# Output projection of a two-layer GLA/MLA trunk: seven products of halves per 1024 tokens in place of eight

## The chip, the cores and the metric

One core of one Trainium2 chip runs the whole program. The metric is the device time of one execution in microseconds (us), taken as the median of several runs.

## The reference

Two layers; the change touches only the last line of each:

```python
for l in range(DEPTH):                       # DEPTH = 2
    h = rmsnorm(x, norm_g[l])
    z = h @ w_in[l]                          # split into the parts of two head groups
    ...
    o_gla = gla_mix(...) * silu(g_gate)      # (1, 2048, 512)
    o_mla = block_causal_attention(q, k, v) * silu(m_gate)   # (1, 2048, 512)
    x = x + jnp.concatenate([o_gla, o_mla], axis=-1) @ w_out[l]   # w_out[l]: 1024 x 1024
```

All arrays are float32; x has 2048 tokens of 1024 features.

## The kernel before, in words

A layer has four stages: `pass1` (input projections and the gated linear attention), `pass2` (gates, queries, the output of the first head group), `phase_b` (softmax attention of the second group) and `phase_c` (the output projection, L1179 to L1303). Arrays that pass from stage to stage lie in DRAM: `yd[q]` holds the input of the output projection, transposed, for a quarter `q` of 512 tokens, as 8 blocks `k` of 128 features; `xd[q]` holds the residual stream after a layer, `sd[q]` its sums of squares.

Every matrix product is made of three matmuls (`mm3`, L98 to L101): an operand is split into a high part, rounded by ACT (type float32r), and a low part, the rest, by DVE (`V`) or POOL (`G`); the matmuls are high times high, high times low and low times high. A weight block of 128 x 512 thus costs a load, an ACT operation and a DVE or POOL one; a block of `y` likewise (`ysplit`, L1207).

`phase_c` runs over 4 quarters `q` and in each over 8 blocks `m` of 128 output features. `part` (L1220) makes one block: 8 blocks `k` of input features, three matmuls each, into one of four PSUM banks (`co`). `done` (L1229) evicts it: DVE adds the residual block `xc`, which was loaded from DRAM by `xload`, and stores the sum to `xd` (layer 0) or to the output (layer 1). In layer 0 it also squares the sum on ACT and adds it to `ac` on POOL (L1242). In the first quarter three banks are begun with `k` 0 to 3, whose `y` was split in `phase_b` (`ypre`, L1162).

All of `w_out` is split ahead of the stage, near the end of `phase_b` (`load_wo`, L1121 and L1158 to L1160), into units of 128 x 4 x 512 from a pool of 12 (`unit`, L91). In layer 0 `phase_c` also loads and splits the next layer's weights `mi` and `qk` (`wpieces`, L236, through `wi_pieces`), normalises the first quarter (`norm0`) and makes the first two hidden tiles (`prep_x`, `prep_h`).

The order of TensorE's instructions in `phase_c` is the order of the program (`manual_schedule`, L1310); on DVE, ACT, POOL and on SP, which issues every DMA (L60), a scheduler orders them ahead of the run, by what is ready and which buffers are free. A pool's tile with a tag and `bufs=n` has n buffers, and an instruction that needs a new one waits for the last use of an old one. Pools `wc` and the PSUM pool exist only in `phase_c`; `hp`, whose two `hT` buffers hold hidden tiles, lasts through the kernel.

## Time and profile before

| | |
|---|---|
| median of 3 runs | 2283.54 us (2283.3 to 2286.54) |
| the profiled execution | 2282.41 us |
| its span, first to last instruction | 2280.6 us |
| around the span | 1.8 us |
| granted TensorE clock | 0.997 of full speed |

The profile is one execution; its sums are held against 2282.41 us. Busy times of an engine are sums of its instructions' durations. PE is TensorE's matmuls, PEld its weight loads, SPq the queue of SP, which issues the DMAs. An instruction's line is that of the helper that emits it: the projection's matmuls stand at L99, L100 and L101 with the tile `co`, its evictions at L1231, the splits of `y` at L1210 and L1211. What follows `<-` in brackets is what an idle engine waited for.

### The profile page before, as it was taken

The numbers are of one execution on the slowest core, as the hardware profiler recorded it, in microseconds if no ns is written. First come the engines' busy times: TensorE is split into PE (matmuls) and PEld (weight loads), VectorE is DVE, ScalarE is ACT, GpSimd is POOL, SyncE is SP. The second block draws the span as 40 slices with busy tenths as digits, with TensorE's granted clock in tenths as the row PEclk, the third lists the DMA queues.
The fourth block names the chain that finished last, engine by engine and source line by source line (L and its number), as shares of the span: only waits on it lengthen the run. The fifth ranks groups of instructions, "written<-read, shape, count | busy, mean of one in ns | idle before, by whom it ended". The sixth has DMA issues, their size and how long they took to land.

```text
span 2280.6 us, 37201 instructions
## 1 busy us (share of the span) xinstructions
PE 2230.0 (98%) x12597; PEld 1927.8 (85%) x12597; DVE 1443.4 (63%) x4421; ACT 1321.4 (58%) x3624; POOL 424.2 (19%) x627
## 2 busy tenths in 40 slices
PE   7999999999999999999999999999999999999999
PEld 5788888888899998888878888888888999988887
DVE  5565557676788888632345555677778888785221
ACT  6655456766777777632244445567777777676100
POOL 0000002334221112232200000044342222123000
PEclk9999999999999999999999999999999999999999
DMA  5410124443311111275421011244432111113542
GB/s 194 142 48 32 43 67 137 127 139 96 107 32 52 36 42 56 65 221 176 139 93 47 29 47 42 71 144 140 124 100 89 37 46 42 36 53 107 178 134 83
DMA packets 168607, 204.78 MB, mean 90 GB/s; under 512 B 12560, under 2 KB 123232, under 8 KB 168416
## 3 DMA queue, kind: packets, MB, share of 16 engines
q1 hardware_dynamic: 168416, 202.40, 28.1%
q8 instruction: 100, 1.64, 0.3%
q14 instruction: 91, 0.75, 0.1%
HBM read 138.39 MB, written 63.96 MB: 89 GB/s over the span
## 4 chain that ended last, share of the span: by engine, by line
PE 86%; ACT 5%; DVE 4%; DMA 3%; issue 1%; POOL 1%; SPq 0%; ACTq 0%; POOLq 0%; DVEq 0%
PE tp L96 8%; PE co L101 5%; PE co L99 5%; PE co L100 5%; PE sp L987 3%; PE sp L990 3%; PE sp L991 3%; PE gt L101 3%; PE gt L100 3%; PE gt L99 3%; PE sp L988 2%; PE o L1062 2%; PE sp L989 2%; PE o L1061 2%; PE mg L101 2%; PE mg L99 2%
## 5 line engine op out<-in xcount | busy, mean ns | idle before, releaser
L100 PE MATMUL co<-y,wo_h 128*128 128x512 f32 x512 | 199.5, 390 | 0.4 <-POOL y L1168 0.4
L99 PE MATMUL co<-y,wo_h 128*128 128x512 f32 x512 | 199.7, 390 | 0.0
L101 PE MATMUL co<-y,wo_l 128*128 128x512 f32 x512 | 199.4, 389 | 0.0
L998 DVE TENSOR_SCALAR_CACHE_REDUCE p<-sp 128x512 f32<-128x512 f32 (+5 forms) x304 | 173.2, 574 | 21.9 <-PE sp L991 18.0
L1005 ACT ACTIVATE p<-p,nm 128x128 f32<-128x128 f32 (+15 forms) x128 | 153.8, 1202 | 36.2 <-DVE nm L1004 31.1
L1040 ACT ACTIVATE ph<-tp 128x512 fp32r<-128x512 f32 x224 | 130.4, 593 | 75.5 <-PE tp L96 67.1
L1041 DVE TENSOR_TENSOR pl<-tp,ph 128x512 fp32r<-128x512 f32 x224 | 151.9, 687 | 33.9 <-ACT ph L1040 32.6
L1060 PE MATMUL o<-ph,v 128*128 128x256 f32 x576 | 168.2, 292 | 4.6 <-ACT ph L1040 3.1
L1062 PE MATMUL o<-pl,v 128*128 128x256 f32 x576 | 170.5, 296 | 2.0 <-DVE pl L1041 1.5
L1231 DVE TENSOR_TENSOR xc<-co,xc 128x512 f32<-128x512 f32 x64 | 44.2, 690 | 202.4 <-PE co L101 201.1
L96 PE MATMUL tp<-cst,p 128*128 128x128 f32 x1088 | 166.2, 275 | 0.5 <-DVE pl L1041 0.2
L1061 PE MATMUL o<-ph,v 128*128 128x256 f32 x576 | 161.4, 280 | 0.0
L186 POOL TENSOR_TENSOR ropeu<-kpe,cos 128x256 f32<-128x256 f32 x8 | 6.8, 846 | 715.0 <-DVE Z L549 714.7
L987 PE MATMUL sp<-kn,q 128*128 128x512 f32 (+3 forms) x320 | 129.6, 405 | 7.1 <-ACT q L922 4.9
L96 PEld LDWEIGHTS tp<-cst,p 128*128 128x128 f32 x1088 | 124.8, 141 | 8.9 <-ACT p L1005 1.3
L1060 PEld LDWEIGHTS o<-ph,v 128*128 128x128 f32 x576 | 109.3, 190 | 12.2 <-ACT ph L1040 5.3
L988 PE MATMUL sp<-kn,q 128*128 128x512 f32 (+3 forms) x320 | 116.5, 364 | 0.0
L989 PE MATMUL sp<-kn,q 128*128 128x512 f32 (+3 forms) x320 | 116.5, 370 | 0.0
L990 PE MATMUL sp<-kr,q 128*128 128x512 f32 (+3 forms) x320 | 115.2, 367 | 0.8 <-ACT q L937 0.4
L1062 PEld LDWEIGHTS o<-pl,v 128*128 128x128 f32 x576 | 109.0, 189 | 7.6 <-DVE pl L1041 3.4
L991 PE MATMUL sp<-kr,q 128*128 128x512 f32 (+3 forms) x320 | 114.2, 367 | 0.0
L100 PEld LDWEIGHTS co<-y,wo_h 128*128 128x128 f32 x512 | 96.2, 188 | 20.8 <-POOL y L1168 0.9
(282 smaller groups left out, 6734.2 us busy)
## 6 DMA issues: line engine op xcount, KB each, us to landing
yst<-yd SPq DMA_DIRECT2D x28, 512.0 KB, 5.0
qd<-qs SPq DMA_DIRECT2D x32, 384.0 KB, 2.9
gst<-qd SPq DMA_DIRECT2D x64, 192.0 KB, 2.5
xn<-in_x SPq DMA_DIRECT2D x16, 512.0 KB, 3.3
od<-osn SPq DMA_DIRECT2D x32, 256.0 KB, 2.1
hf<-in_xt SPq DMA_DIRECT2D x16, 512.0 KB, 3.5
on<-od SPq DMA_DIRECT2D x32, 256.0 KB, 2.7
yd<-yT SPq DMA_DIRECT2D x32, 256.0 KB, 2.8
```

The source lines that it names most:

```text
L96: T.transpose(o, i, ident[:k, :k])
L99: T.matmul(o, lhsT=lh, rhs=rh, start=start, stop=False)
L100: T.matmul(o, lhsT=lh, rhs=rl, start=False, stop=False)
L101: T.matmul(o, lhsT=ll, rhs=rh, start=False, stop=stop)
L987: T.matmul(o, lhsT=qn[:, 0, ts_], rhs=kn[:, 0, k0:k1], start=True, stop=False)
L988: T.matmul(o, lhsT=qn[:, 0, ts_], rhs=kn[:, 1, k0:k1], start=False, stop=False)
L990: T.matmul(o, lhsT=qrr[:, 0, ts_], rhs=kr[:, c0:c1], start=False, stop=False)
L991: T.matmul(o, lhsT=qrr[:, 1, ts_], rhs=kr[:, c0:c1], start=False, stop=True)
L998: V.tensor_scalar(out=pt[:, c0:c0 + w], in0=sp[:, 0:w], scalar1=0.0, scalar2=-3e38, op0=ALU.add, op1=ALU.max, accum_out=mx[:, m:m + 1])
L1060: T.matmul(o[:, s], lhsT=vh, rhs=ph[:, j, s], start=(kb == 0), stop=False)
L1061: T.matmul(o[:, s], lhsT=vl, rhs=ph[:, j, s], start=False, stop=False)
L1062: T.matmul(o[:, s], lhsT=vh, rhs=pl[:, j, s], start=False, stop=(last and j == 1))
```

## The change

The 1024 x 1024 weight is cut into four quarters A11, A12, A21, A22 (input half by row, output half by column; the first input half is scaled by a gain `g`), and the input for 1024 tokens, a pair of quarters q0, q1, into the four halves of 512 features by 512 tokens. Seven products of a weight combination and an input combination take the place of eight: M1 (A11), M5 (S1), M6 (N2), M7 (S3), M3 (S4), M2 (A12), M4 (A22), in this order (`prods`, `left`).

Each product has 4 output blocks `i`, 4 blocks `k` and three matmuls each, `k` outermost (in the very last product `i`). M1, M6, M7 and M4 use the same four banks (`ca`), the first fresh, the others adding to what stands there; M5 and M3 use four others (`cb`), M3 adding; M2 starts those afresh. Every product is evicted by DVE with an added operand: after M1, M5 and M6 a residual block is added and the sum goes to a scratch array `sc` in DRAM; after M7, M3 and M2 the operand is that scratch block, read back, and the sum is final; after M4 the operand is a residual block and the sum final.

Of the weights only A11 and S1 are made in `phase_b`; N2, S3, S4, A12 and A22 are made during the first pair, block by block (`n2`, `s3`, `s4`, `a22`), each from `w_out` loaded anew. The right sides are made and split (`right`, `rput`) one product ahead; the raw halves `ra`, `rb` of `y` are loaded into the two `hT` buffers and are changed in place, other blocks come through `cload`. The next layer's weights are loaded one block at a time, with every second block on POOL alone (the condition in `wpieces`), in the second pair.

The core of the diff, without the removed body of `phase_c`:

```diff
-                    if lo is G and k % 2 == 1:
+                    if lo is G and (k0 + k) % 2 == 1:
...
-            def load_wo(c, half, lo=None):
-                wo[c] = wchunk(lambda hf, k0: bpl.tile([P, 512], F32, tag="stg", name="stg", bufs=NSTG).unsqueeze(1),
-                               1, w_out[l], [(0, c * 512, 512)], 512, f"wo{c}_{l}", ("gla", sm["glag"]), lo,
-                               us=wo.get(c), halves=(half,))
+            def wtile():
+                return bpl.tile([P, 512], F32, tag="stg", name="stg", bufs=NSTG)
+            def load_a11():
+                us = wchunk(lambda hf, k0: wtile().unsqueeze(1), 1, w_out[l], [(0, 0, 512)], 512, f"A11{l}",
+                            ("gla", sm["glag"]), G, halves=(0,))
+                wo["A11"] = us["h", 0], us["l", 0]
+            def load_s1():
+                hi, lo = wo["S1"] = unit([P, 4, 512], F32R, f"S1h{l}"), unit([P, 4, 512], F32R, f"S1l{l}")
+                for k in range(4):
+                    t, u = wtile(), wtile()
+                    dma(t, w_out[l][k * P:(k + 1) * P, 512:1024])
+                    dma(u, w_out[l][512 + k * P:512 + (k + 1) * P, 512:1024])
+                    V.scalar_tensor_tensor(out=u, in0=t, scalar=sm["glag"], in1=u, op0=ALU.mult, op1=ALU.add)
+                    A.activation(out=hi[:, k, :], in_=u, func=AF.Copy)
+                    G.tensor_tensor(out=lo[:, k, :], in0=u, in1=hi[:, k, :].bitcast(F32), op=ALU.subtract)
...
-                    load_wo(0, 0, G)
+                    load_a11()
...
-            load_wo(0, 1, G)
-            load_wo(1, 0)
-            load_wo(1, 1, G)
+            load_s1()
...
     def phase_c(l, wc, pp, yu):
         more = l + 1 < DEPTH
         if more:
             layer_g8(l + 1)
             layer_small(l + 1)
+        g = smalls[l]["glag"]
+        hT01, ac = {}, {}
+        rh, ops, banks = {}, {}, {}
+        prods = ["M1", "M5", "M6", "M7", "M3", "M2", "M4"]
+        left = {"M1": "A11", "M5": "S1", "M6": "N2", "M7": "S3", "M3": "S4", "M2": "A12", "M4": "A22"}
+        W = wo
+        def wtile():
+            return wc.tile([P, 512], F32, tag="ws", name="ws", bufs=6)
+        def wload(c, r):
+            t = wtile()
+            dma(t, w_out[l][r * P:(r + 1) * P, c * 512:(c + 1) * 512])
+            return t
+        def wput(name, k, t, lo, scale=None):
+            hi, ll = W[name][0][:, k, :], W[name][1][:, k, :]
+            if scale is None:
+                A.activation(out=hi, in_=t, func=AF.Copy)
+                lo.tensor_tensor(out=ll, in0=t, in1=hi.bitcast(F32), op=ALU.subtract)
+            else:
+                A.activation(out=hi, in_=t, func=AF.Copy, scale=scale)
+                V.scalar_tensor_tensor(out=ll, in0=t, scalar=scale, in1=hi.bitcast(F32), op0=ALU.mult,
+                                       op1=ALU.subtract)
+        def wmake(name):
+            if name not in W:
+                new = (lambda n: wc.tile([P, 4, 512], F32R, tag="wx", name=n, bufs=2)) if name == "A22" else \
+                    (lambda n: unit([P, 4, 512], F32R, n))
+                W[name] = new(f"{name}h{l}"), new(f"{name}l{l}")
+        def n2(k):
+            wmake("N2")
+            t = wload(0, k)
+            V.scalar_tensor_tensor(out=t, in0=t, scalar=g, in1=W["S1"][0][:, k, :].bitcast(F32), op0=ALU.mult,
+                                   op1=ALU.subtract)
+            V.tensor_tensor(out=t, in0=t, in1=W["S1"][1][:, k, :].bitcast(F32), op=ALU.subtract)
+            wput("N2", k, t, G)
+        def s3(k):
+            wmake("S3")
+            t, u = wload(0, k), wload(1, k)
+            G.tensor_tensor(out=t, in0=t, in1=u, op=ALU.subtract)
+            wput("S3", k, t, None, g)
+        def s4(k):
+            wmake("A12")
+            wmake("S4")
+            t = wload(0, 4 + k)
+            wput("A12", k, t, G)
+            for part in range(2):
+                G.tensor_tensor(out=t, in0=t, in1=W["N2"][part][:, k, :].bitcast(F32), op=ALU.add)
+            wput("S4", k, t, G)
+        def a22(k):
+            wmake("A22")
+            wput("A22", k, wload(1, 4 + k), G)
+        ra, rb, rc = {}, {}, {}
+        def yload(q, half):
+            t = hp.tile([P, 4, 512], F32, tag="hT", name="yr")
+            dma(t, yd[q][:, 4 * half:4 * half + 4, :])
+            return t
+        def cload(p, j, q, k):
+            t = rc[p, j, k % 4] = wc.tile([P, 512], F32, tag="rc", name="rc", bufs=4)
+            dma(t, yd[q][:, k, :])
+        def rput(p, j, k, t):
+            y = rh[p, j, k] = wc.tile([P, 2, QD], F32R, tag="y", name="y", bufs=6)
+            A.activation(out=y[:, 0, :], in_=t, func=AF.Copy)
+            V.tensor_tensor(out=y[:, 1, :], in0=t, in1=y[:, 0, :].bitcast(F32), op=ALU.subtract)
+        def fetch(p, j, k):
+            q0, q1 = 2 * p, 2 * p + 1
+            name = prods[j]
+            if name == "M1" and p > 0:
+                cload(p, j, q0, k)
+            elif name in ("M6", "M3"):
+                cload(p, j, q1, 4 + k)
+            elif name == "M2":
+                cload(p, j, q0, 4 + k)
+        def right(p, j, k):
+            name = prods[j]
+            tt = lambda o, a, b, op: V.tensor_tensor(out=o, in0=a, in1=b, op=op)
+            if name == "M1":
+                if p == 0:
+                    rh[p, j, k] = yu[k // 2][:, k % 2]
+                    return
+                t = rc.pop((p, j, k))
+            elif name == "M5":
+                t = ra[p][:, k, :]
+                tt(t, rb[p][:, k, :], t, ALU.subtract)
+            elif name == "M6":
+                t, b, c = ra[p][:, k, :], rb[p][:, k, :], rc.pop((p, j, k))
+                tt(t, t, c, ALU.subtract)
+                tt(b, c, b, ALU.subtract)
+            elif name == "M7":
+                t = rb[p][:, k, :]
+            elif name == "M3":
+                t = rc.pop((p, j, k))
+            elif name == "M2":
+                t, a = rc.pop((p, j, k)), ra[p][:, k, :]
+                tt(a, a, t, ALU.add)
+            else:
+                t = ra[p][:, k, :]
+            rput(p, j, k, t)
...
+        def place(p, name, i):
+            q0, q1 = 2 * p, 2 * p + 1
+            return {"M1": (q0, i), "M5": (q1, 4 + i), "M6": (q1, i), "M7": (q1, 4 + i), "M3": (q1, i),
+                    "M2": (q0, i), "M4": (q0, 4 + i)}[name]
+        adds = {"M7": "M5", "M3": "M6", "M2": "M1"}
+        def opload(p, j, i):
+            name = prods[j]
+            q, m = place(p, name, i)
+            t = ops[p, j, i] = wc.tile([P, QD], F32, tag="xc", name="xc", bufs=7)
+            if name in adds:
+                dma(t, sc[adds[name], i])
+            elif l == 0:
+                dma(t, x0[:, m, q * QD:(q + 1) * QD])
+            else:
+                dma(t.rearrange("p (a c) -> p a c", a=4), xd[q][:, :, m, :])
+        def evict(p, j, i, ps):
+            name = prods[j]
+            q, m = place(p, name, i)
+            t = ops.pop((p, j, i))
+            V.tensor_tensor(out=t, in0=ps, in1=t, op=ALU.add)
+            if (name, i) in sc:
+                dma(sc[name, i], t)
+                return
...
+            n = ac.setdefault(q, [0, None])
+            n[0] += 1
+            if n[0] == 1:
+                n[1] = wc.tile([P, QD], F32, tag="ac", name="ac", bufs=1)
+                A.activation(out=n[1], in_=t, func=AF.Square)
+                return
+            sq = wc.tile([P, QD], F32, tag="sq", name="sq", bufs=1)
+            A.activation(out=sq, in_=t, func=AF.Square)
+            G.tensor_tensor(out=n[1], in0=n[1], in1=sq, op=ALU.add)
+            if n[0] == KT:
+                dma(sd[q], n[1])
...
+        go = lambda f, *a: (lambda: f(*a))
+        jobs = {}
+        def at(p, j, k, *fs):
+            jobs.setdefault((p, j, k), []).extend(fs)
+        for k in range(4):
+            at(0, 0, k, go(n2, k))
+            at(0, 1 + k // 2, k % 2 * 2, go(s3, k))
+            at(0, 2 + k // 2, k % 2 * 2 + 1, go(s4, k))
+            at(0, 4, k, go(a22, k))
+        if more:
+            for n, which in enumerate(("mi", "qk")):
...
+                at(1, 2 + 2 * n, 0, begin)
+                for i in range(8):
+                    at(1, 2 + 2 * n + i // 4, i % 4, go(piece, i))
+            for t in range(2):
+                for half in range(2):
+                    at(1, 5, 3, go(prep_x, t, half))
+                    at(1, 6, 1 + t, go(prep_h, t, half))
+            at(1, 6, 0, norm0)
+        seq = [(p, j) for p in range(2) for j in range(7)]
+        ra[0], rb[0] = yload(0, 0), yload(1, 0)
+        for i in range(4):
+            opload(0, 0, i)
+        for k in range(4):
+            right(0, 0, k)
+        for n, (p, j) in enumerate(seq):
+            name = prods[j]
+            nxt = seq[n + 1] if n + 1 < len(seq) else None
+            tag = "cb" if name in ("M5", "M3", "M2") else "ca"
+            fresh = name in ("M1", "M5", "M2")
+            for i in range(4):
+                if fresh:
+                    banks[tag, i] = pp.tile([P, 512], F32, tag=tag, name="co", bufs=4)
+            wh, wl = W[left[name]]
+            def step(k):
+                if nxt:
+                    if k == 0:
...
+                        for kk in range(4):
+                            fetch(*nxt, kk)
+                        right(*nxt, 0)
+                        right(*nxt, 1)
+                    elif k < 3:
+                        right(*nxt, k + 1)
+                    opload(*nxt, k)
+                if name == "M4" and p == 0 and k == 0:
+                    rb[1], ra[1] = yload(3, 0), yload(2, 0)
+                for f in jobs.get((p, j, k), ()):
+                    f()
+            def mul(i, k):
+                cs = slice(i * P, (i + 1) * P)
+                y = rh[p, j, k]
+                o = banks[tag, i]
+                for a, b, c in ((wh, 0, 0), (wh, 1, 1), (wl, 0, 2)):
+                    T.matmul(o, lhsT=a[:, k, cs], rhs=y[:, b, :], start=(fresh and k == 0 and c == 0),
+                             stop=(k == 3 and c == 2), skip_group_check=True)
+            if nxt:
+                for k in range(4):
+                    for i in range(4):
+                        mul(i, k)
+                        if i == 0:
+                            step(k)
+                        if k == 3:
+                            evict(p, j, i, banks[tag, i])
             else:
+                for i in range(4):
                     for k in range(4):
+                        mul(i, k)
+                        if k == 0:
+                            step(i)
+                    evict(p, j, i, banks[tag, i])
...
```

## Rows read from the trace of the kernel before

**Rows 1.** The page: busy time by engine, and the chain that ended last.
```profile
PE 2230.0 (98%) x12597; PEld 1927.8 (85%) x12597; DVE 1443.4 (63%) x4421; ACT 1321.4 (58%) x3624; POOL 424.2 (19%) x627
...
PE 86%; ACT 5%; DVE 4%; DMA 3%; issue 1%; POOL 1%; SPq 0%; ACTq 0%; POOLq 0%; DVEq 0%
```

**Rows 2.** Busy time by stretch: output projection of layer 0, then layer 1.
```profile
core 0: us, PE busy (x) PEld busy (x) DVE busy (x) ACT busy (x) POOL busy (x), PEclk, DMA share, GB/s
975.05:1150.50 175.45, 175.27 (x777) 145.03 (x777) 55.93 (x81) 47.94 (x82) 51.04 (x38) 1.00 0.55 172
...
2101.40:2277.30 175.90, 174.67 (x769) 144.04 (x769) 37.11 (x52) 17.66 (x29) 14.54 (x11) 1.00 0.43 137
```

**Rows 3.** Tile co: ns min/median/max; waits before its instructions (us, times).
```profile
L99 PE MATMUL co<-y,wo_h x512: 388/390/486, 975.1 to 2275.6; 128*128 128x512 f32 x171
...
L1231 DVE TENSOR_TENSOR xc<-co,xc x64: 677/692/692, 987.4 to 2276.5; 128x512 f32<-128x512 f32 x64
...
  PE co L101: 201.1, 51
...
  POOL y L1168: 1.3, 2
  DMA yst<-yd: 1.2, 1
```

**Rows 4.** Timeline of TensorE, layer 0's projection: start us, duration us.
```profile
975.80 0.39 PE L99 MATMUL co<-y,wo_h 128*128 128x512 f32 x1
976.03 0.39 PE L100 MATMUL co<-y,wo_h 128*128 128x512 f32 x1
976.26 0.39 PE L101 MATMUL co<-y,wo_l 128*128 128x512 f32 x1
...
999.60 0.39 PE L99 MATMUL co<-y,wo_h 128*128 128x512 f32 x1
```

**Rows 5.** Timeline of SP's DMA issues: at the start, and in layer 0's projection.
```profile
20.28 0.82 SPq L60 DMA_DIRECT2D pk<-in_smalls  x2
...
976.08 0.92 SPq L60 DMA_DIRECT2D yst<-yd  x2
...
988.08 0.52 SPq L60 DMA_DIRECT2D xd<-xc  x1
...
990.93 0.33 SPq L60 DMA_DIRECT2D xc<-in_xT  x1
```

**Rows 6.** Timeline of DVE, layer 0's projection.
```profile
981.52 2.62 DVE L1211 TENSOR_TENSOR y<-yst,y 128x512 fp32r<-128x512 f32 x4 [5.84 <-ACT y L1210]
...
990.33 1.37 DVE L1211 TENSOR_TENSOR y<-yst,y 128x512 fp32r<-128x512 f32 x1
991.64 0.69 DVE L1231 TENSOR_TENSOR xc<-co,xc 128x512 f32<-128x512 f32 x1
```

**Rows 7.** Timeline of POOL, the same stretch.
```profile
989.85 1.29 POOL L1211 TENSOR_TENSOR y<-yst,y 128x512 fp32r<-128x512 f32 x1 [1.22 <-ACT y L1210]
991.12 1.72 POOL L1242 TENSOR_TENSOR ac<-ac,sq 128x512 f32<-128x512 f32 x1
```

**Rows 8.** Groups by line in 975 to 1145 us: busy us, mean ns.
```profile
L1211 POOL TENSOR_TENSOR y<-yst,y 128x512 fp32r<-128x512 f32 x9 | 14.3, 1594 | 16.0 <-DMA yst<-yd 10.7 <-ACT y L1210 5.3
...
L267 DVE SCALAR_TENSOR_TENSOR wqk_l<-stg,pk,wqk_h 128x512 fp32r<-128x512 f32 x8 | 5.6, 746 | 3.7 <-ACT wqk_h L266 3.7
...
L352 DVE TENSOR_TENSOR hT<-xt,hT 128x512 fp32r<-128x512 f32 x4 | 3.3, 855 | 10.2 <-ACT hT L351 10.2
```

**Rows 9.** Timeline at the end of layer 0's projection.
```profile
1149.93 0.39 PE L101 MATMUL co<-y,wo_l 128*128 128x512 f32 x1
1150.36 0.69 DVE L1231 TENSOR_TENSOR xc<-co,xc 128x512 f32<-128x512 f32 x1 [4.75 <-PE co L101]
...
1151.10 0.47 PE L99 MATMUL mi<-wmi_h,hT 128*128 128x464 f32 x1 [0.78 <-DVE xc L1231]
```

**Rows 10.** DMA of both stages: layer 0, its issues (us to landing), layer 1.
```profile
DMA packets 25674, 30.22 MB, mean 172 GB/s; under 512 B 1472, under 2 KB 18496, under 8 KB 25664
...
xc<-in_xT SPq DMA_DIRECT2D x32, 256.0 KB, 2.7
xd<-xc SPq DMA_DIRECT2D x31, 256.0 KB, 2.8
...
DMA packets 23579, 24.17 MB, mean 137 GB/s; under 512 B 1264, under 2 KB 17776, under 8 KB 23572
```

**Rows 11.** Busy time by stretch, layer 0's projection (columns of rows 2).
```profile
975.00:981.00 6.00, 6.00 (x27) 4.99 (x28) 0.42 (x1) 0.41 (x2) 1.35 (x2) 1.00 0.64 193
981.00:988.00 7.00, 7.00 (x32) 5.81 (x31) 3.83 (x6) 3.77 (x7) 0.67 (x1) 1.00 0.98 367
988.00:994.00 6.00, 6.00 (x28) 4.95 (x28) 4.17 (x6) 2.92 (x6) 3.62 (x3) 1.00 0.79 227
994.00:1000.00 6.00, 6.00 (x28) 4.99 (x27) 3.17 (x4) 3.04 (x5) 1.29 (x1) 1.00 0.86 260
```

**Rows 12.** DMA issues in 976 to 988 us.
```profile
xc<-in_xT SPq DMA_DIRECT2D x4, 256.0 KB, 6.0
```

130 lines of the change are left out of this document (27 added, 103 removed).

## The prediction

> **What bounds the kernel now.** I read first the page's busy times and its chain of waits [rows 1]: TensorE is busy for 98% of the span and holds 86% of the chain that ended last. That share is an average over stages, so next the two output projections by themselves: the stretch table [rows 2] gives 175.45 us and 175.90 us, in which TensorE is busy all the time while DVE, ACT and POOL are at a third or less; the DMA engines stand at 0.55 and 0.43. Nothing but TensorE's own stream ends these stages: before the projection's matmuls the tile view finds 2.5 us of waits in all (1.3 for POOL, 1.2 for a DMA), while DVE waits 201.1 us for TensorE [rows 3]. So a matmul taken out is time won, as long as the other engines keep up.
>
> What a matmul is worth must not be read from its duration. The tile view says 390 ns [rows 3], but the timeline starts 35 groups of three between 975.80 and 999.60 [rows 4]: 23.80 us / 105 = 0.2267 us each; 768 of them are 174.1 us, which is the stage. The durations overlap. The Trainium skill ("TensorE: Matmul & The Clock Gate", section "Back-to-back issue gap") gives about 131 ns for a sustained 512-column matmul; by it the 192 matmuls below would be worth an estimated 25 us. The rows say 227 ns, and the measurement decides.
>
> **The change part by part.** *Matmuls.* Before, a layer has 4 x 8 x 8 x 3 = 768; after, 14 products of 4 x 4 x 3 = 48, so 672. Two layers lose 192 x 0.2267 = **43.5 us**. A product lasts 10.88 us, a pair of quarters (seven products) 76.2 us, a layer 152.4 us.
>
> *Work at the end of attention.* Twelve weight loads with their splits (12 ACT, 8 POOL, 4 DVE) become eight loads with 4 ACT, 4 POOL and 4 DVE operations. I take 0: TensorE waits there for transposes and softmax, not for these; what less there is to do can only help, by under 1 us (the wait before the projection now is the 1.3 us of [rows 3]).
>
> *Start.* M1 needs the y units that are made already, and four banks at once where three served. The raw y tiles for M5 are in the long-lived pool; the queue issues a load as soon as its tile is free, however far ahead: the next layer's `pk` loads, written in this phase, went out at 20.28 us [rows 5]. So these 2 MB and the four subtractions of M5 should be done during attention: 0. The weight tiles for N2 are in the phase's own pool and are loaded only then, as `yst` is now, at 976.08 us [rows 5]. N2 needs a load, three DVE/POOL operations and an ACT one per block by M6 at 21.8 us, beside the operands of M6: 0 to 4 us, I take 2 a layer.
>
> *DVE and POOL together.* This is the large cost. While POOL subtracted from 989.85 to 991.14, a DVE subtraction with both inputs in SBUF took 1.37 us instead of 0.66 (four in 2.62 us, when POOL was still), and POOL's next add took 1.72 instead of 1.29 [rows 6, 7]: the two wait for each other. An eviction, whose one input is PSUM, ran at 991.64 in its usual 0.69 while POOL was busy. So I add DVE's two-SBUF-input operations (0.66) and POOL's (1.29) as one queue, and leave the evictions out. Under the first pair come 28 low parts of right sides (the next pair's M1 among them), 12 sums for M6 and M2, 8 operations for N2, 4 for S3: 52 x 0.66 = 34.3 us; POOL has 4 for N2, 4 for S3, 16 for S4 and A12, 4 for A22: 28 x 1.29 = 36.1 us, and in layer 0 also 10 sums of squares, 12.9 us. That is 70.4 us in layer 1 and **83.3 us in layer 0, against 76.2**. The deadline that bites first is M3, whose last quarter starts at 4 x 10.88 + 3 x 2.72 = 51.7 us and needs S4's last block. By then 36 DVE (M5, M6, M7, M3 low parts, M6's sums, N2, S3) and 24 POOL operations are due: 23.8 + 31.0 = 54.8 us, 58.6 with three sums of squares, from about 1 us on. That is late by 4 us in layer 1 and 8 us in layer 0. The later deadlines of layer 0 add nothing to this 8. Bounds: 0, if both queues overlap freely, as an operation and an eviction do; above, the low-part row on POOL under contention, 1.594 us instead of 1.29 [rows 8], which makes 24 x 0.3 = 7 us more a layer. I take the solo durations, because in one queue waiting is already counted. In the second pair layer 0 has 40 x 0.66 + 8 x 0.75 + 4 x 0.86 (next layer's weights and hidden tiles) [rows 8] = 35.8, and POOL 16 + 14 operations, 38.7: 74.5 of 76.2 us, no loss; layer 1 has only 26.4.
>
> *Evictions.* There are 56 a layer instead of 32, at 0.69 [rows 3]: 38.6 us of DVE, beside TensorE. But M7 follows M6 into the same banks, M2 follows M3, and the next M1 follows M4: five hand-overs a layer. At the stage's end now, a matmul that starts at 1149.93 lets the next one go at 1151.10, after the eviction [rows 9]: 1.17 us. The new order leaves nine matmuls of other banks in between, 2.04 us, so 0.87 us spare. A DVE that has one operation in front and waits for POOL is late by 0.66 + 1.29 = 1.95 us: 0 to 1.1 us per place. I take 1.1 in layer 0 (5.5 us) and half in layer 1 (2.7 us).
>
> *Transfers.* The first pair moves 104 blocks of 0.262 MB: 32 operand loads, 16 and 8 of y, 20 of weights, 28 stores: 27.3 MB; the second pair 16.8 MB, and 22.6 in layer 0 with next weights and hidden tiles. Now a whole stage moves 30.2 and 24.2 MB [rows 10]. When 98% busy the engines carried 367 GB/s [rows 11]: 27.3 MB take 74.4 us, just under the 76.2 of TensorE and under the delayed 84. I take 0 and keep the slower flows for a rival. The Trainium skill ("HBM Reference", section "Specifications (TRN2)") gives about 358 GB/s as a core's share; by it the first pair would take an estimated 76.3 us, the same as TensorE. The row is a little higher, with one core running. Issuing costs 0.33 to 0.52 us each [rows 5], some 40 us of SP's 76.
>
> *Sum.* Losses: layer 0 8 + 5.5 + 2, layer 1 4 + 2.7 + 2, together 24.2 us. 2282.4 - 43.5 + 24.2 = 2263.1 us against the profiled execution, which is 1.1 us below the median of the runs: **2264 us**. With the small ends (8 + 4 alone) it is 2252, with the large ones (12 + 11 + 8) 2271.
>
> **Rivals.** *All hides* (15%): POOL's and DVE's operations interleave better than one queue, since much of this work has no producer but a load and can run early. Then only 0 to 6 us of the 43.5 are lost: 2241 to 2247. For it: the early loads of [rows 5]. Against: [rows 6, 7].
>
> *The transfers become the bound* (20%), and the change is slower. Place: the first pair of both layers and the second of layer 0, where every load and store goes through SP in order, and a load that waits for a buffer holds back those behind it. The four stretches of [rows 11] are the busiest 25 us now, and move (6 x 193 + 7 x 367 + 6 x 227 + 6 x 260) / 25 = 266 GB/s. If that is all that the queue can sustain, 27.3 + 27.3 + 22.6 MB take 290 us, and with 76.2 us for layer 1's second pair the stages last 366 us against 351.4: 15 us slower, 2298 us. It decides below 77.2 MB / (351.4 - 76.2) = 280 GB/s. Against it: those 25 us contain the first 3 us of an empty queue, and 367 GB/s in the middle.
>
> *The operand ring* (15%). Seven `xc` buffers serve four blocks a product: a product's fourth operand can be loaded only when the product before has stored its first. That store starts about 0.9 us before the product ends; store and load take 2.8 + 2.7 us as medians over the stage [rows 10], and the block then lands well in time; but in the loaded start four loads took 6.0 us [rows 12]. With 6 us each way the block lands 11 us into a product of 10.88. Each 0.5 to 1 us over, in 28 products, takes 14 to 28 us from the forecast: 2278 to 2292.
>
> **How the numbers follow.** The forecast has 50%, and its own range is 2252 to 2271. The range of 8 in 10 reaches from 2245 (half of "all hides" left out) to 2298 (half of the transfer case). Some 0.2%, 4.6 us, is what a measurement can tell from no change. Faster by more: 50 + 15 and 5 of the ring's 15, 70%; within it: 8% from the ring; slower: 20% and 2 from the ring, 22%.
>
> **What would show it.** Right: 1344 projection matmuls 0.227 us apart; stages of about 168 us in layer 0 and 161 in layer 1; TensorE's waits lying in the first pair at M3's last blocks, on POOL's S4 low parts, and at the starts of M7 and M2 on DVE; DVE's low parts of right sides near 1.3 us on average in the first pair. Wrong: waits on DMA at evictions or before right sides (transfers, ring), a DMA share near 1 through both pairs, or no waits at all. A granted clock under 1.00 in these stages would break the price of a matmul itself.

## The result, and the profile after

The change makes the kernel slower: 2314.6 us median of 4 runs (2313.6 to 2320.43) against 2283.9 us (2283.3 to 2286.54) in the same session, ratio 1.0137 with a 95% interval of 1.0119 to 1.0156, some 31 us. The forecast was 2264 us, faster than before; the measured time is slower than before and lies outside the range of 2245 to 2298. The profiled execution took 2314.62 us with a span of 2312.5.

The page, beside [rows 1]: TensorE executes the 192 matmuls fewer but is busy only 16 us less, and its share of the chain has fallen from 86% to 76%.

```profile
PE 2214.1 (96%) x12405; PEld 1906.6 (82%) x12405; DVE 1602.4 (69%) x4615; ACT 1364.9 (59%) x3696; POOL 502.6 (22%) x673
...
PE 76%; DVE 7%; DMA 6%; ACT 4%; issue 3%; POOL 3%; SPq 1%; DVEq 0%; POOLq 0%; ACTq 0%
```

From the first to the last projection matmul a stage takes 194.2 us in layer 0 and 179.3 in layer 1; before it was 175.1 and 174.9, and the new matmuls alone are 152.4. So 41.8 and 26.9 us are lost within the stages, 68.7 in all; another 8.5 us lie outside them (4.7 before layer 0's stage, 4.1 between the stages, 0.3 won at the end). In the stretch table of layer 0 (columns as in [rows 2]) each line is one product: M1, M5, M6, M7, M3, M2, M4, then the second pair's M1 and, further down, its M3, M2 and M4.

```profile
979.75:990.74 10.99, 10.99 (x50) 9.07 (x50) 4.48 (x8) 1.85 (x4) 0.00 (x0) 1.00 0.80 264
990.74:1001.62 10.88, 10.88 (x49) 9.01 (x48) 10.88 (x14) 3.58 (x6) 5.68 (x4) 1.00 0.94 339
1001.62:1020.98 19.36, 13.82 (x50) 10.84 (x49) 17.40 (x22) 7.82 (x13) 8.82 (x8) 0.82 0.84 284
1020.98:1037.23 16.25, 13.05 (x50) 9.98 (x48) 9.57 (x10) 5.30 (x10) 16.25 (x12) 0.89 0.84 299
1037.23:1051.46 14.23, 11.38 (x49) 8.77 (x48) 11.79 (x13) 6.63 (x12) 14.23 (x10) 1.00 0.87 270
1051.46:1062.90 11.44, 11.26 (x49) 9.01 (x50) 6.20 (x9) 4.72 (x8) 9.95 (x8) 1.00 0.91 291
1062.90:1075.26 12.36, 11.04 (x49) 8.85 (x48) 9.72 (x15) 4.72 (x8) 3.62 (x4) 1.00 1.01 341
1075.26:1092.20 16.94, 13.22 (x48) 9.91 (x49) 13.63 (x17) 5.46 (x9) 7.54 (x6) 0.90 0.74 229
...
1124.90:1140.00 15.10, 11.04 (x50) 8.85 (x48) 15.10 (x17) 8.00 (x15) 8.93 (x6) 0.98 0.74 233
1140.00:1152.30 12.30, 12.30 (x48) 10.07 (x49) 7.35 (x12) 5.68 (x10) 5.19 (x4) 0.88 0.63 193
1152.30:1173.90 21.60, 15.69 (x57) 12.69 (x56) 4.30 (x14) 4.19 (x9) 7.37 (x6) 0.76 0.36 106
```

A product that waits for nothing takes 10.88 us, as forecast. The worst are M6 and M7 (DVE busy all through M5 and for 17.4 us of M6, POOL all through M7 and M3), the hand-over from M4 to the next M1, and the last M4. Layer 1 reads 10.99, 10.88, 19.86, 16.21, 12.78, 11.44, 17.83, then 13.99 and six times 10.88. The projection's waits of TensorE took 2.5 us before [rows 3]; in the list of waits (us in total, times, longest) these are the largest now:

```profile
PE co L1448 <- DVE xc L1339: 24.5, 13, 6.8
PE co L1448 <- DVE y L1273: 11.3, 2, 5.8
...
PE co L365 <- DMA ss<-sd: 5.9, 1, 5.9
...
PE co L1448 <- POOL S4l L1217: 2.2, 2, 1.1
```

They are 44 us of the 68.7. Most of the rest is in the granted clock of the table, 0.76 to 0.90 in the products with the longer waits: by the timeline, 99 matmuls of the two stages started some 0.42 us behind the one before instead of 0.227, which is 20 us. TensorE's timeline at M6 of layer 1 shows it, and so do two stretches of the same product (columns as above, the granted clock third from the end):

```profile
2157.31 0.80 PE L1448 MATMUL co<-y,N2h 128*128 128x512 f32 x1 [5.79 <-DVE y L1273]
...
2158.34 1.05 PE L1448 MATMUL co<-y,N2h 128*128 128x512 f32 x2
...
2159.61 1.05 PE L1448 MATMUL co<-y,N2h 128*128 128x512 f32 x2
...
2164.18 0.62 PE L1448 MATMUL co<-y,N2h 128*128 128x512 f32 x2
...
2164.87 0.62 PE L1448 MATMUL co<-y,N2h 128*128 128x512 f32 x2
...
2157.31:2163.45 6.14, 6.14 (x14) 4.79 (x15) 6.14 (x9) 1.10 (x3) 1.09 (x1) 0.50 0.86 309
2163.45:2171.00 7.55, 7.55 (x34) 6.22 (x33) 5.42 (x8) 3.24 (x6) 3.93 (x4) 1.00 0.89 275
```

After the wait a group of three starts every 1.27 us, 0.42 us a matmul, at a granted clock of 0.50 (the 1.2 GHz level); from 2163.45 on the clock is 1.00 (2.4 GHz) and a group soon starts every 0.69 us. The 5.79 us of waiting became 8.98 lost in the product.

Who was late is in DVE's timeline of layer 0 between M5 and M6:

```profile
989.05 0.75 DVE L1233 SCALAR_TENSOR_TENSOR ws<-ws,pk,S1h 128x512 f32<-128x512 f32 x1 [6.27 <-DMA ws<-in_w_out]
...
996.60 1.63 DVE L1288 TENSOR_TENSOR yr<-yr,rc 128x512 f32<-128x512 f32 x1
...
1000.56 1.78 DVE L1288 TENSOR_TENSOR yr<-yr,rc 128x512 f32<-128x512 f32 x1
1002.26 1.75 DVE L1288 TENSOR_TENSOR yr<-rc,yr 128x512 f32<-128x512 f32 x1
...
1005.74 3.44 DVE L1273 TENSOR_TENSOR y<-yr,y 128x512 fp32r<-128x512 f32 x2
```

DVE idles until N2's first load lands, 9.3 us into the stage, and then never stops: eight operations for N2, eight sums and four evictions stand ahead of M6's first low part at 1005.74. M6's first matmul, which needs high parts alone, ran at 1001.62; the next one waited for this. Where POOL runs beside it an operation takes 1.2 to 1.8 us instead of 0.68.

M7 of layer 0 shows the next step. M6's last eviction stands behind two operations that ran beside POOL, and TensorE waits 2.98 us for it (2.96 in layer 1, behind the same two):

```profile
1022.50 1.83 DVE L1220 SCALAR_TENSOR_TENSOR S3l<-ws,pk,S3h 128x512 fp32r<-128x512 f32 x1
1024.26 1.75 DVE L1273 TENSOR_TENSOR y<-rc,y 128x512 fp32r<-128x512 f32 x1
1025.93 0.68 DVE L1339 TENSOR_TENSOR xc<-co,xc 128x512 f32<-128x512 f32 x1
```

At M4 to M1 in layer 1 POOL has nothing, and the eviction that TensorE waits for stands in DVE's order behind sums whose loads are late:

```profile
2218.09 2.50 DVE L1288 TENSOR_TENSOR yr<-yr 128x512 f32<-128x512 f32 x4 [5.41 <-DMA yr<-yd]
...
2226.44 0.69 DVE L1288 TENSOR_TENSOR yr<-rc,yr 128x512 f32<-128x512 f32 x1 [3.44 <-DMA rc<-yd]
2227.83 0.69 DVE L1288 TENSOR_TENSOR yr<-rc,yr 128x512 f32<-128x512 f32 x1 [0.70 <-DMA rc<-yd]
2228.44 0.68 DVE L1339 TENSOR_TENSOR xc<-co,xc 128x512 f32<-128x512 f32 x1
```

### The profile page after: what moved, and what is told of

It reads as the page before. It is cut to its first block, busy times and chain, and to the rows that moved or that the text cites. A ratio compares the mean times of both kernels' runs of the same rounds, so it can differ in the third digit from the quotient of the medians.

```text
span 2312.5 us, 37493 instructions
## 1 busy us (share of the span) xinstructions
PE 2214.1 (96%) x12405; PEld 1906.6 (82%) x12405; DVE 1602.4 (69%) x4615; ACT 1364.9 (59%) x3696; POOL 502.6 (22%) x673
## 4 chain that ended last, share of the span: by engine, by line
PE 76%; DVE 7%; DMA 6%; ACT 4%; issue 3%; POOL 3%; SPq 1%; DVEq 0%; POOLq 0%; ACTq 0%
PE tp L95 8%; PE co L1448 6%; PE o L1061 3%; PE sp L986 3%; PE o L1060 3%; PE sp L989 2%; PE o L1059 2%; PE sp L990 2%; PE sp L987 2%; PE sp L988 2%; PE mg L100 2%; PE mg L98 2%; PE mg L99 2%; PE gt L100 2%; PE gt L99 2%
## 5 line engine op out<-in xcount | busy, mean ns | idle before, releaser
L997 DVE TENSOR_SCALAR_CACHE_REDUCE p<-sp 128x512 f32<-128x512 f32 (+5 forms) x304 | 173.1, 573 | 23.1 <-PE sp L990 18.2
L1018 POOL TENSOR_SCALAR gt<-gt,rl 128x128 f32<-128x128 f32 x128 | 80.2, 636 | 184.9 <-DVE rl L1016 116.8
L1059 PEld LDWEIGHTS o<-ph,v 128*128 128x128 f32 x576 | 108.9, 189 | 9.5 <-DVE yT L1071 2.9
L903 POOL TENSOR_SCALAR gst<-kpe,rk 128x64 f32<-128x64 f32 x128 | 55.3, 446 | 278.0 <-DVE rk L111 108.9
L1060 PEld LDWEIGHTS o<-ph,v 128*128 128x128 f32 x576 | 108.8, 189 | 2.3
L98 PE MATMUL vp<-wv_h,hT 128*128 128x512 f32 x256 | 108.8, 425 | 1.8 <-ACT wv_h L265 1.8
L98 PE MATMUL qk<-wqk_h,hT 128*128 128x512 f32 x256 | 109.5, 428 | 0.0
```

Source lines behind the costliest of these rows:

```text
L98: T.matmul(o, lhsT=lh, rhs=rh, start=start, stop=False)
L997: V.tensor_scalar(out=pt[:, c0:c0 + w], in0=sp[:, 0:w], scalar1=0.0, scalar2=-3e38, op0=ALU.add, op1=ALU.max, accum_out=mx[:, m:m + 1])
L1059: T.matmul(o[:, s], lhsT=vh, rhs=ph[:, j, s], start=(kb == 0), stop=False)
L1060: T.matmul(o[:, s], lhsT=vl, rhs=ph[:, j, s], start=False, stop=False)
```

## The experiments

Each kernel ran once with a profile, beside a run of the kernel before on the same chip (2283 to 2287 us), the two with an interval in several rounds. "Stages" are layer 0's and layer 1's in us, as above (194.2 and 179.3 in the change). A product's time runs to the start of the next one, so a wait of that one's first matmul is in it. One run is little for a total: ten runs of a single kernel below lay between 2285.9 and 2294.9 us. Products are firmer: those that the first edit below leaves alone moved by less than 2 us. Where an edit has more lines than are shown, "..." marks it.

**norm0 later.**

```diff
-            at(1, 6, 0, norm0)
+            at(1, 6, 3, norm0)
```

> Layer 0's last product takes 21.6 us in the changed kernel, of which TensorE waits 5.9 us for the sums of squares that norm0 needs and then runs at a lower clock. Here norm0's eight matmuls stand behind the third quarter of that product instead of the first. If that wait is the cause: the last product 11 to 13 us and the whole 2303 to 2306 us. If something else is late there too (evictions, transfers): the product stays above 16 us and the whole above 2309 us.

2301.2 us, stages 183.3 and 177.0; the last M4 of layer 0 falls from 21.6 to 11.8. `norm0`'s eight small matmuls stood in TensorE's order behind the first group of that product and waited 5.9 us for the sums of squares to come back from DRAM. That cost of 10 us is shown. The whole fell by 13, but 2 of these lie in layer 1, which the edit does not touch.

**DVE in program order in the projection.**

```diff
-                    tc.manual_schedule(engines=PEO):
+                    tc.manual_schedule(engines=PEO | {mybir.EngineType.DVE}):
```

> DVE executes the projection stage in the order of the program instead of the scheduler's. Theory 1 (DVE's queue: sums made early stand in front of the low parts and evictions that are due): M6 of either layer loses its 5.5 us wait and takes 11 to 14 us instead of 19.4 and 19.9, layer 1's M4 and the M1 after it 11 to 14 instead of 17.8 and 14.0; the whole 2280 to 2298 us. Theory 2 (amount of work on DVE and POOL, which wait for each other): the work is the same, M6 stays above 17 us and the whole within 6 us of 2314.6 or above it. Theory 3 (transfers late): as theory 2.

2302.1 us, stages 193.1 and 172.7. In layer 1 everything from M3 on takes 10.88: the hand-overs are a matter of DVE's order. But M6 grows to 27.0 and 25.3. DVE stands idle for N2's first load as in the change (5.9 us in layer 1, 6.2 there), now with low parts of M5 behind it; and TensorE waits 9.4 us in layer 1 for M6's evictions, which program order puts behind low parts of S3 and of M7's right sides.

**No weights made.**

```diff
-        left = {"M1": "A11", "M5": "S1", "M6": "N2", "M7": "S3", "M3": "S4", "M2": "A12", "M4": "A22"}
+        left = {"M1": "A11", "M5": "S1", "M6": "A11", "M7": "S1", "M3": "A11", "M2": "S1", "M4": "A11"}
...
-            at(0, 0, k, go(n2, k))
...
-            at(0, 4, k, go(a22, k))
```

> N2, S3, S4, A12 and A22 are not made: all products use A11 or S1, which exist. 20 loads, 12 DVE, 28 POOL and 20 ACT operations fall away in the first pair of a layer. Theory 2 (work on DVE and POOL) and theory 3 (transfers; 84 blocks instead of 104 in the pair): the first pairs fall from 95.5 and 100 us (M1 to M4) to 78 to 84, the whole to 2270 to 2282. Theory 1 (queue order, loads late in front of evictions): M6, M7 and M3 recover but the losses at M4 and the following M1 stay (7 to 10 us a layer), the whole 2284 to 2292.

2282.4 us, stages 174.7 and 168.3: 19.5 and 11.0 us less, 30.5 of the 68.7. M6 has 17.3 of them (11.0 and 10.9 now); the others are M7 in layer 1 (5.3), M3 in layer 0 (3.4) and, in layer 0's second pair, M1, M3 and M2 (8.5), less what other products lost. M7 of layer 0 did not fall (17.3), and in layer 1 M4 and M1 stay (33.7 us for two). M3 and M2 of layer 0's second pair take 10.88 each:

```profile
1109.73:1120.61 10.88, 10.88 (x50) 9.01 (x48) 8.52 (x13) 5.47 (x9) 4.49 (x4) 1.00 0.69 196
1120.61:1131.49 10.88, 10.88 (x50) 9.01 (x48) 6.06 (x10) 4.91 (x9) 4.82 (x4) 1.00 0.71 217
```

In this run DVE's low parts of the next layer's weights started at 998 to 1021 us, under the first pair; in the change at 1093 to 1133, under the second.

**POOL's weight work as copies on ACT.**

```diff
-                lo.tensor_tensor(out=ll, in0=t, in1=hi.bitcast(F32), op=ALU.subtract)
+                A.activation(out=ll, in_=t, func=AF.Copy, scale=2.0 ** -12)
...
```

> Every POOL operation of the weight making (S3's difference, S4's two sums, the low parts of N2, A12, S4 and A22: 28 a layer) is replaced by one plain copy on ACT of the same size, so N2, S3, S4, A12 and A22 don't hold the right values; loads, DVE operations and matmuls are as in the change; the sums of squares stay on POOL. Theory POOL (DVE and POOL wait for each other, and POOL's own queue is late for S4): in layer 1, where POOL then has nothing, the products M7 (16.2 us), M3 (12.8), M2 (11.4) come down to about 10.9 each and M6 (19.9) to about 15, so layer 1's stage 179.3 -> 163 to 169 us; layer 0 8 to 14 us shorter; time about 2290 to 2298. Rival, the loads and DVE's own order: M6 stays above 18, M7 above 14, M4 and the next M1 together above 30, and layer 1's stage stays within 5 us of 179; time above 2305.

2289.7 us, stages 181.6 and 167.7. M6 falls to 11.5 and 11.8, M3 to 10.9, and DVE's low parts in layer 1 from averages of 0.75 and 0.97 us (two groups) to 0.69: without POOL, M6 is nearly in time although DVE idles as long for N2's first load (6.5 us). M7 stays late at 18.0 and 17.8, so POOL is not all; there, in layer 1, an eviction waited 3.75 us for its operand:

```profile
2156.64 0.69 DVE L1339 TENSOR_TENSOR xc<-co,xc 128x512 f32<-128x512 f32 x1 [3.75 <-DMA xc<-xd]
```

**No weight loads.**

```diff
-            t = wtile()
-            dma(t, w_out[l][r * P:(r + 1) * P, c * 512:(c + 1) * 512])
-            return t
+            return wtile(), W["A11" if c == 0 else "S1"][0][:, r % 4, :].bitcast(F32)
...
```

> The 20 weight loads a layer of the projection stage are left out (5.2 MB a layer); the weight making does the same operations on the same engines, but on weights that lie in SBUF already, so N2, S3, S4, A12 and A22 don't hold the right values. Theory late loads (N2's first load goes out 3.5 us into the stage and lands 5 us later, and DVE then has everything at once): M6's wait of 5.5 and 5.8 us goes, M6 19.4 and 19.9 -> 11 to 14 us, M7 16 -> 11 to 14; time 2296 to 2303. Theory of the transfers as the bound (the queue and the DMA engines carry too much): in addition the waits of M4 and the next M1 (12.4 + 17.0 and 17.8 + 14.0 us) fall to about 22 to 24 a pair, and the time falls to 2285 to 2293. Theory DVE and POOL (too much work in the first half of the pair, whatever the loads): M6 and M7 together stay above 30 us, time above 2308.

2309.4 us; M6 and M7 together 35.4 and 36.9 us. So late weight loads and their traffic are not enough to explain this loss: with the inputs in place M6 is later still (23.9 and 22.2).

**N2 early; and the same with DVE in program order.** Both have `norm0` later too.

```diff
+                    dma(v, w_out[l][k * P:(k + 1) * P, 0:512])
+                    V.scalar_tensor_tensor(out=v, in0=v, scalar=sm["glag"], in1=u, op0=ALU.mult, op1=ALU.subtract)
...
-            at(0, 0, k, go(n2, k))
...
```

> N2 is made at the end of attention beside S1 (one DVE operation, one ACT copy and one POOL low part a block, from the raw S1 tile), so four loads and eight DVE operations leave the first pair's start; norm0 three steps later as in the run before. Theory late loads and DVE's load at M6: M6 19.4 / 19.9 -> 11 to 13 us, M7 less too; layer 0's stage 183 -> 171 to 176, layer 1's 177 -> 164 to 170, with 0 to 2 us more at the end of attention; time 2284 to 2292. Rival DVE and POOL: the 16 S4 and S3 operations on POOL still come before M3, so what M6 loses no more comes back at M7 and M3, and the time stays above 2296.

> As the run before, and DVE follows program order in the projection stage. Theory late loads plus order: with N2 out of the way program order has no late operation in front, so M5 and M6 stay at about 11 to 13 us, M7 to M1' at about 11, as those were in the run with program order alone; layer 0's stage 165 to 172, layer 1's 155 to 160; time 2264 to 2276. Rival: DVE in order now waits for POOL's S3 and S4 differences, M7 or M3 is 5 to 15 us late, time 2285 to 2300.

2297.3 us (stages 175.4, 170.2) and 2287.2 us (173.1, 165.1). M6 is cured in the first (11.7, 11.2), but M7 stays late (18.6 and 16.6, after 17.9 and 16.3 with `norm0` later alone). Against that run the two stages are 14.7 us shorter and the whole only 3.9: layer 0's stage begins 7.4 us later and the stretch between the stages is 3.6 longer. So most of what M6 won seems to be paid at the end of attention, where N2 is now made; single runs do not show this firmly. With program order too, M6 and M7 take 32 to 34 us together and the rest of layer 1 10.9 each. There SP's issues stand still in layer 1: from 2143 to 2155 SP waits 4.2 us for DVE's operations on S3's low parts, which hold weight tiles, and 2.9 for one on a right side. These operations take 1.75 us each beside POOL, which is busy without a break from 2142 to 2170. M6's fourth operand (`xc<-xd`) is behind them, and its eviction waits 4.5 us for it:

```profile
2145.39 3.90 SPq L59 DMA_DIRECT2D ws<-in_w_out  x2
2152.26 0.33 SPq L59 DMA_DIRECT2D yr<-yd  x1
2153.93 0.33 SPq L59 DMA_DIRECT2D ws<-in_w_out  x1
2154.31 0.52 SPq L59 DMA_DIRECT2D xc<-xd  x1
...
2160.22 0.69 DVE L1345 TENSOR_TENSOR xc<-co,xc 128x512 f32<-128x512 f32 x1 [4.52 <-DMA xc<-xd]
```

**The weight work of POOL on DVE: alone; with N2 early and DVE in program order; and with all else of POOL's on DVE too.**

```diff
-            wput("N2", k, t, G)
+            wput("N2", k, t, V)
...
```

> The 28 POOL operations a layer of the weight making (S3's difference, S4's two sums, the low parts of N2, A12, S4, A22) are done by DVE, with the same operands; everything else as in the change, the sums of squares stay on POOL. Theory of one queue (DVE and POOL don't run operations with two SBUF inputs side by side, so POOL's 1.29 us is taken from DVE, and the same operation on DVE takes 0.66): the first pair's 36 us of POOL become 18.5 us of DVE, DVE's other operations fall back to about 0.68 us, M6 19.4 / 19.9 -> 14 to 17 us, M7 and M3 fall by 1 to 4 each; layer 1's stage 179 -> 163 to 170, layer 0's 194 -> 178 to 186; time 2285 to 2297. Rival, the engines overlap and DVE is simply the busier one: 18.5 us more on the engine that is late already, M6 to M3 each later than now, time above 2318. Rival, transfers: no change within 5 us, 2309 to 2319.

> N2 made early, norm0 late and DVE in program order as in the run before (2287), and in addition the weight making's POOL operations done by DVE. Theory of one queue: layer 1's stage 165 -> 153 to 158 us (a pair is 76.2 of matmuls; DVE then has 38 evictions and low parts, sums and weights, some 62 us, under the first); layer 0's 173 -> 162 to 168, what is left being M3 and M2 of the second pair; time 2264 to 2278. Rival, transfers and SP's order: the fourth operand of M6 still lands late (M6 and M7 together above 30 us in layer 1), time 2280 to 2290.

> As the run before, and POOL has nothing left in the projection stages: the next layer's weight pieces and the sums of squares go to DVE too (a sum one eviction later, with two square tiles instead of one and five weight tiles instead of six). Theory of one queue: M3 (15.6 us) and M2 (13.1) of layer 0's second pair fall to about 11 each, so layer 0's stage is 5 to 8 us shorter than in the run before, and layer 1's the same; time 2257 to 2272. Rival: what holds M2 there is ACT, whose copies stand behind the squares, or the loads of hidden tiles and weights: the stage falls by less than 2 us.

Alone 2301.8 us (stages 187.8, 169.4), 13 us less than the change and 5 above the expected top: in layer 1 DVE's low parts of right sides and its sums are back at 0.68 to 0.69 us on average, and M6 is at 14.8 and 15.1, but M3 now waits for S4 on DVE (20.8, 16.2). With N2 early and in program order it is a miss, 2297.7: DVE stands at the weight operations, whose ACT halves wait for loads issued in the same step (3.4 us at one block of A12), and M6 rises to 24. The third, 2297.4, misses as well: M3 and M2 of layer 0's second pair keep 16.0 and 13.8 without POOL, so POOL alone is not what holds them. ACT's timeline there shows a copy of the next layer's weights waiting for its load, with a right side's copy behind it:

```profile
1128.25 0.72 ACT L265 ACTIVATE wqk_h<-ws,pk 128x512 fp32r<-128x512 f32 x1 [5.47 <-DMA ws<-in_w_qk]
1128.88 0.61 ACT L1278 ACTIVATE y<-rc 128x512 fp32r<-128x512 f32 x1
```

**No scratch traffic.**

```diff
             if name in adds:
-                dma(t, sc[adds[name], i])
+                return
...
             if (name, i) in sc:
-                dma(sc[name, i], t)
                 return
```

> M1, M5 and M6 of each pair are not stored to the scratch in DRAM and not read back: M7, M3 and M2 add a resident tile in their place, so parts of the sum are left out; 48 of the layer's blocks of 0.26 MB fall away, 24 in each pair, all else as in the change. Theory of one queue: M6 stays at 18 to 20 us and M7 above 14, the wait of M1 of the second pair in layer 1 (6.8 us) shrinks by at most half; time 2302 to 2314. Theory of transfers and the operand ring: M7, M3, M2 and the next M1 fall to about 11 to 12 us, 2280 to 2295.

2321.7 us, no faster, with 12.5 MB a layer fewer (layer 0's stage 37.6 MB at a share of 0.58, against 50.1 MB at 0.78). That rules the amount of transfers out as the bound. M3 of layer 0 takes 21.5 us here, and TensorE's waits for POOL's S4 are 8.3 us in all instead of 2.2; why was not pursued.

**Loads ahead of their use; DVE free; stores on POOL's queue; loads ahead and stores on POOL's queue.**

```diff
+            at(0, 1, k, go(wget, ("a", k), 0, 4 + k))
+            at(0, n // 4, n % 4, go(hi_, "A12", k, ("a", k)))
+            at(0, (n + 1) // 4, (n + 1) % 4, go(s4a, k))
...
```

> N2 and S3 made at the end of attention; norm0 late; DVE in program order; A12's and A22's raw blocks are loaded one product before DVE's operations on them, S4, A12 and A22 are made on DVE alone, and the next layer's weight pieces are loaded three steps before they are split. Theory of operations standing behind a late load: with the loads ahead, M6 and M7 are 11 to 13 us each in layer 1 (24.0 and 12.7 in the run with DVE in order and loads at their use), M2 of layer 0's second pair about 11 (13.3); stages 158 to 165 and 153 to 157; time 2257 to 2270. Theory of too much work for DVE: M6 and M7 together above 28 us, time above 2280. Theory of SP's queue (loads late behind stores, whatever their place): waits at M7 of 3 to 8 us stay, 2272 to 2285.

> The run before with DVE in the scheduler's order, as in the change. If the order was harmful only because of late loads, the two agree within 5 us; if the scheduler puts evictions behind sums, as at M4 and the next M1 in the change, those two products are 4 to 10 us longer a layer in layer 1, and the time is 5 to 15 us above the run before.

> The change with one edit: the 56 stores a layer of evicted blocks are issued by POOL's queue instead of SP's. Theory of SP's queue: loads no longer stand behind stores; the waits <- DMA of DVE shrink, M7 (16 us) and the M4 to M1 hand-over (12.4 + 17.0, 17.8 + 14.0) fall by 3 to 8 us each place, time 2285 to 2300. Theory of work and order: no change but what the issues cost POOL, 2310 to 2325 (POOL, late in M3 already, stands behind each store's eviction: M3 longer).

> Loads ahead as in the first of these runs, and the stores issued by POOL's queue. Theory of operations behind late loads alone: within 4 us of the first. Theory of SP's queue: 6 to 15 us less than the first, down to 2250 to 2262, with products of M6, M7, M2 at 10.9 to 11.5.

The first took 2294.5 us against an expected 2257 to 2270, and its layer 1 is the most telling: thirteen products at full clock with TensorE never idle, after a first one that waited 12.5 us for its y units (M3 and M2 of layer 0's second pair stay at 18.5 and 12.8).

```profile
2132.04:2147.00 14.96, 14.41 (x49) 11.29 (x50) 7.08 (x10) 4.43 (x8) 5.02 (x4) 0.75 0.88 278
2147.00:2288.40 141.40, 141.40 (x625) 116.93 (x623) 95.72 (x149) 36.90 (x60) 0.00 (x0) 1.00 0.79 262
```

So the engines can do what is left in the stage in time, with N2 and S3 made ahead of it; but the twelve weight blocks now stood ahead of the y units, which cost 12.5 us and a first product 4.1 us longer. With DVE in the scheduler's order, all else the same, it is 2319.8: M4 and M1 take 30.5 and 33.1 us together instead of 25.2 and 21.8, the effect of order alone. Stores on POOL's queue cost 37 us (2351.6). An issue holds POOL for 0.55 us, and POOL sat idle 101 us in layer 1's stretch before its stores, waiting for evictions, with its weight work behind them in order; this is the likely cause, but no run takes it apart. Loads ahead and stores on POOL's queue together take 2314.9, 20 more than loads ahead alone, where at most 4 more were expected. A queue that is free is no place for an instruction that must wait for another engine.

**Everything placed; y units first.** Two more attempts at the first of these: S3 made under M1 to M6 again, with its loads two or three steps ahead; and the y units loaded before the weights.

```diff
+        for k, n in enumerate((0, 1, 5, 6)):
+            on(n, go(wget, ("c", k), 0, k), go(wget, ("d", k), 1, k))
...
```

> As the run with loads ahead and DVE in program order, but S3 is made in the projection again (loads under M1 and M5, operations two or three steps later), so that nothing new stands before the y units; the next layer's weight pieces are split on ACT and DVE alone, so POOL has only the sums of squares; two accumulators for these in place of one, five weight tiles in place of six. Theory that the order and place of loads made the loss: no wait before the first matmul, layer 1's stage 152.4 to 156 us, layer 0's 156 to 164; time 2250 to 2264, so 20 to 35 us faster than before. Theory that the engines and transfers can't carry this work: S3 back in the projection costs M6 and M7 5 us or more a layer, time 2268 to 2285.

> The run with loads ahead (N2 and S3 made at the end of attention, DVE in program order), but the y units are loaded and split before S1, S3 and N2; the next layer's weight pieces on ACT and DVE alone; two accumulators for the sums of squares, five weight tiles. Theory that places of loads made the loss: the first matmul no longer waits (before: 12 us), M5, M6 and M7 within 1.5 us of 10.9 since S1, N2 and S3 have 11, 22 and 33 us; layer 1's stage 153 to 157, layer 0's 155 to 163; time 2250 to 2266. Rival, the twelve weight loads of 3.1 MB only move the wait: S1 late at M5 by 5 us or more, or the operands of M1 late behind them; time 2270 to 2285.

The first: 2289.8 us, ratio to before 1.0016 (1.0006 to 1.0027), stages 178.9 and 165.5, with M6 and M3 at 16 to 20 us again. It lies above what either theory expected, and so does the second: 2298.95 us, ratio 1.0060 (1.0043 to 1.0076); M5 now waits 9.2 and 8.4 us for its right side. Wherever the weight making was put, it made the next thing late. No version with the whole arithmetic beat the kernel before. The best two, N2 early with DVE in order (one run, 2287.2 us) and everything placed (2289.8), each end some 4 us behind the kernel before in their own sessions.

**Three parts off at once.** No weights made, norm0 late and DVE in program order, the three edits above together.

> N2, S3, S4, A12 and A22 are not made (products use A11 and S1 in their place, so five of seven products have other left sides), norm0 stands after the last product, DVE in program order. Theory that these three make up the loss: layer 1's stage 152.4 to 154 us, layer 0's 157 to 162 (M3 and M2 of its second pair still late, 13.2 + 13.1 us in the run without weights, other work being untouched there); time 2248 to 2258. If transfers or the work on right sides alone are a bound, M7 (17.3 us in layer 0, 12.6 at M3 and 13.1 at M2 in layer 1 in the run without weights) stays above 13 in program order too: 2262 or more.

2255.6 us, 59 less than the change. Layer 1's projection waits for nothing and is the sum of its matmuls, at 254 GB/s:

```profile
2097.43:2249.90 152.47, 152.47 (x674) 126.00 (x673) 90.60 (x139) 32.20 (x51) 0.00 (x0) 1.00 0.78 254
```

Layer 0 takes 163.8, with M4 and M1 at 25.7 and the second pair's M3 and M2 at 15.6 and 12.6. So these three parts together hold 57 of the 68.7 us lost in the stages; 11 stay, all in layer 0. The expectation above gives M3 and M2 of layer 0's second pair as 13.2 and 13.1 us in the run without weights; by that run's rows they took 10.88 each. With DVE in program order the low parts of the next layer's `qk` weights stand under the second pair again (1110 to 1131 us), which fits; no run moved them alone.

## Why the prediction was wrong

The forecast losses and the measured ones, by place (us, layer 0 and layer 1; measured is a product's time over 10.88):

| place | forecast | measured |
|---|---|---|
| M6: N2 and its right side in time | 2, 2 | 8.5, 9.0 |
| M3: S4 in time | 8, 4 | 3.4, 1.9 |
| hand-overs, five a layer: | 5.5, 2.7 | |
| - M7 | | 5.4, 5.3 |
| - M2, M4 and the next M1 | | 8.1, 10.6 |
| - M3 and M2 of the second pair | | 5.7, 0 |
| last M4 (`norm0`) | 0 | 10.7, 0 |

**The matmuls: right.** 672 a layer, 0.2267 us apart, 10.88 a product; the run with three parts off gives layer 1 152.47 us, forecast 152.4.

**DVE and POOL: the step that failed.** The mechanism was right: the two wait for each other, and the move of POOL's work to DVE took that away. The Trainium skill ("SBUF — State Buffer", section "SBUF: two separate sides") calls the port pair that they share an exclusive lock, held for a whole instruction; rows with 1.75 us for DVE beside POOL agree. The size is smaller than forecast: the low parts of right sides took 1.0 and 0.9 us on average in the first pair, forecast 1.3. What failed is where the queue was held against a deadline. The prediction took M3's deadline as the first to bite and added the queue up to it from 1 us on, without evictions: 8 and 4 us, where TensorE waited 1.1 and 1.1 for S4. For N2 at M6 it allowed 2 us a layer, and worked out no queue for it. The deadline that bites first is M6: its sums, its low parts, N2's operations and four evictions are all due in some 12 us, after a start at 9.3. Twenty operations stand ahead of M6's first low part: 12 us at 0.6 from start to start, and 16.7 with POOL (989.05 to 1005.74). M6 lost 8.5 and 9.0 us, and comes down to 10.9 to 11.8 without the weight making, without POOL's part of it, or with N2 made early.

**The hand-overs: mis-sized.** "0 to 1.1 us per place" assumed that an eviction has one operation in front. At M7 it had two, each 1.75 us or more beside POOL, for 3.0 us of waiting; at M4 to M1 of layer 1 it had sums that wait for a load, for 6.8 us. With the slow clock behind the waits M7 lost 5.4 and 5.3 us, M4 and M1 7.6 and 10.1. Program order alone cured M4 to M1 of layer 1.

**What was not priced.** `norm0` was taken as part of the work that moves for nothing; in TensorE's order it cost 10 us. And no wait was given its second price: some 20 us went into matmuls at the 1.2 GHz level after waits. The prediction said that a granted clock below 1.00 would break the price of a matmul, but gave its own forecast waits only their length. The Trainium skill ("TensorE: Matmul & The Clock Gate", section "HAM oscillation — how this bites in real kernels") describes this for waits between bursts of matmuls; these rows agree, with 5.79 us of waiting that became 8.98.

**Start, end of attention.** N2's loads were late as feared, but taking all weight loads away won some 5 us only. The end of attention was forecast to cost 0; layer 0's stage begins 4.7 us later and the stretch between the stages is 4.1 longer. Why stays open: in the variants that leave the end of attention as in the change the two vary from 3 to 11 and from -1 to 5, and no run was made for them.

**Rivals.** The transfers fell: the stage's 257 GB/s is under the 280 at which they were to decide, yet 12.5 MB fewer made it no faster, and 254 GB/s went with no wait at all. A rate in a stage that waits says how much was asked for, not what can be carried. The operand ring fell as a first cause: its seven buffers served that last stage without a wait; a late operand was seen in two variants only as one of several waits (3.75 and 4.5 us). No rival held what happened, engine queues in an order that lets one late load stop the work behind it; it stands there only as a price of 1.1 us. Layer 0's M3 and M2 in the second pair stay open in part: more than one wait was seen there (ACT behind a weight load, ACT's single square tile behind POOL). They took 10.88 in one run only, the one without weights, where the next layer's weights were split early; that this is the cause is not shown.

## What to carry to other kernels

Fewer matmuls pay only if their operands exist in time: list, for each product, what every engine must finish before its first matmul, evictions included, and compare with the time since the inputs land, not with the stage's total. On an engine that runs in a fixed order a late load costs all that stands behind it, so issue loads well ahead of the instruction that uses them, and keep instructions that wait for other engines off queues that something needs. Price a wait of TensorE with the slow matmuls behind it.

## What was not expected of the hardware

A stage's matmuls ran at about half rate for some 6 us after a wait of 5.8 us in the middle of dense work (1.27 us per group of three against 0.69, granted clock 0.50). A wait of 3.0 us had slow matmuls behind it too; one of 1.1 us by itself had none. Issuing a store from POOL's queue held POOL for 0.55 us each.
